# One task list for both attentions, two single score banks, and operands that change places

## The chip, the cores and the metric

The kernel runs on one core of one Trainium2 chip. The metric is device time in microseconds. The kernel before takes 2530.77 us, the median of three runs (2530.05 to 2532.8). All other times are from one profiled execution of it.

## The reference

It is one layer of a streaming encoder for 592 tokens: 512 of a prompt with 16 meta tokens in front of them, and 64 further tokens of a running stream, which also reads 128 cached positions. The model width is 2048.

```python
z = rmsnorm(x) @ w_in                       # 3904 columns, all heads
# group A, 8 heads: differential attention, two components of 64
s = q_c @ k_c.T * DIFF_SCALE + bias         # c = 0, 1; T5 relative bias
p = softmax(s_0) - lam * softmax(s_1)
o_d = rmsnorm(p @ v) * (1 - lam_init)
# group B, 8 heads: latent attention
qm  = rmsnorm(z_cq) @ w_uq                  # 128 plain + 64 rotated columns a head
km, vm = rmsnorm(z_ckv) @ w_ukv ; k_rope = rope(z_kr)
o_m = softmax((qn @ km.T + qr @ k_rope.T) * MLA_SCALE) @ vm
x = x + concat(o_d, o_m) @ w_out
x = x + (silu(h @ w_gate) * (h @ w_up)) @ w_down   # h = rmsnorm(x)
```

Attention is causal by chunks of 64. The new keys, values, latents and rotated keys are outputs too.

## The kernel before

All products of the projections and attentions are taken in three matmuls: each float32 operand is split in a high part (a copy on ScalarE, L156) and the rest (a subtraction on VectorE, L153), and high·high, high·low and low·high are summed in PSUM. A projection of 128 output columns reads its weights in two loads of 512 KB (tile `wr`, two buffers, on SP's queue), each split into `wh` and `wl` (two buffers each). Each half feeds 48 matmuls of 128x296, 6 for each of 8 slices of the width. Here "a weight half" is such a load.

**The order of the work.** `Streams` (L46) is a planner that runs while the program is written. Each task is a generator with a rank; the planner holds a clock of its own, runs the ready task of the lowest rank, and advances the clock by a guessed time for each matmul. A task that needs PSUM calls `take("sp")` (scores), `"tp"` (transposes), `"po"` (the output of an attention) or `"ps"` (projections), and hands it back with `give(name, delay)`, where the delay is a guess of when the reader will have finished. What the planner decides is TensorE's order of instructions; it is kept as written. The other engines are put in order by the scheduler of the language, and wait by semaphores, so a wrong guess costs waiting and nothing else. Tasks of low rank are attentions; the task of the highest rank is filler.

**First attention (L325 to L684).** After the norm and the bias tables (built from `oh` and `rbt`, tile `tsk`, pool `xc`), `projections()` (L616) makes queries, keys and values of head after head as filler, and `diff_attend` (L542) runs a head: five blocks of queries b (widths W of 144, 272, 400, 528, and 192 for the stream's tokens), in each the two components c. For each, two matmuls write the score tile `sp`, VectorE adds the bias and takes the minimum (L559, the "reduce" of this document, whose results are `e` and `nm`), ScalarE takes the exponential, and VectorE weighs and subtracts. The score tile is one tile of two banks, of which there is one (pool `pss`, bufs=1):

```python
pss = ph.enter_context(tc.tile_pool(name="pss", bufs=1, space=PSUM, reuse_waits="tile"))
def sbig(name="sp"):
    return pss.tile([P, 2, 512], F32, name=name, tag="sp")
...
st.give("sp", 1.2 + 0.0015 * W)
if c == 0:
    yield 1.2 + 0.0015 * W
```

Block 3 (W = 528) lies in both banks, 264 columns in each. The probabilities are transposed into `tp` and multiplied with the values into `po` (`probabilities_times_values`, L214). The head's norm uses the two-bank score tile too (`pq`). Finished heads go to memory (`mspill`). After head 7 come seven more projections, i in (4, 5, 6, 0, 1, 2, 3), for the latents; then `st.run()` at L684 ends the first list of tasks.

**Second attention (L687 to L973).** New pools are opened. SP loads the rotation matrix `rot` and the tables `cos` and `sin` (L717 to L719), POOL reloads seven heads from `mspill` (L742), and `mix_operand` splits them. `latents()` rotates the shared keys (`pr`) and splits the latents; `heads()` (L952) makes queries and keys of head after head, `latent_attend` scores them (five matmuls a piece, a maximum L928, an exponential L929), and `mix_out()` (L816), the output projection over the first eight heads, is filler. `qsum` (L748) is the sum of squares for the query norm. `mh` and `ml` are the split small weights. A second `st.run()` ends it. The rest of the output projection and the feed-forward part (L1120 to the end) follow.

Of the kernel before, what the change touches and what calls it, by code (L numbers as in the profile page):

```python
# [115 lines left out]
def encoder_step(  # L116
# [14 lines left out]
    wp_cm = tc.tile_pool(name="wp", bufs=2, reuse_waits="tile")  # L131
# [82 lines left out]
    def probabilities_times_values(pt_b, p5, pm, vm, vkeys, vown, vpast, pool, tbank, pso, pace, done, bufs, transposed):  # L214
# [21 lines left out]
        st.give("tp", 1.9)  # L236
        for t in range(2):
# [12 lines left out]
            st.give("tp", 1.9)  # L250
# [34 lines left out]
    def scores(b, sp, parts):  # L285

        if b == 4:
            n, W, q0 = NS, P + NS, 0
            pieces = [(0, 0, W, 0)]
            flat = True  # L290
        else:
            n, W, q0 = P, 144 + P * b, OWN + P * b
            flat = W <= 512
            k0 = PAST + NS
            pieces = [(0, 0, W, k0)] if flat else [(0, 0, W // 2, k0), (1, 0, W // 2, k0 + W // 2)]
        for bank, o, w, k0 in pieces:
            for i, (q, k) in enumerate(parts):
                PE.matmul(sp[0:n, bank, o:o + w], q[:, q0:q0 + n], k[:, k0:k0 + w],
                          start=i == 0, stop=i == len(parts) - 1)
        if flat:  # L300
            return n, W, sp[0:n, 0, 0:W], lambda t: t
        return n, W, sp[0:n, :, 0:W // 2], lambda t: t.rearrange("p (a b) -> p a b", a=2)

# [21 lines left out]
    with ExitStack() as ph:  # L325
        xp = ph.enter_context(tc.tile_pool(name="xp", bufs=1, reuse_waits="tile"))
        az = ph.enter_context(tc.tile_pool(name="az", bufs=1, reuse_waits="tile"))
        pj = ph.enter_context(tc.tile_pool(name="pj", bufs=2, space=PSUM, reuse_waits="tile"))
        pss = ph.enter_context(tc.tile_pool(name="pss", bufs=1, space=PSUM, reuse_waits="tile"))
        pst = ph.enter_context(tc.tile_pool(name="pst", bufs=1, space=PSUM, reuse_waits="tile"))  # L330
        pso = ph.enter_context(tc.tile_pool(name="pso", bufs=1, space=PSUM, reuse_waits="tile"))

# [3 lines left out]
        def sbig(name="sp"):  # L336
            return pss.tile([P, 2, 512], F32, name=name, tag="sp")
# [10 lines left out]
        rb = az.tile([P, T], F32, name="rb")  # L348
# [75 lines left out]
        ap = ph.enter_context(tc.tile_pool(name="ap", bufs=1, reuse_waits="tile"))  # L424

        qs = [[[ap.tile([P, T], F32R, name=f"q{i}{c}{s}") for s in "hl"] for c in range(2)] for i in range(2)]
        pt_b = [ap.tile([P, NM + P * (b + 1)], F32, name=f"p{b}") for b in range(4)]
        pmt = ap.tile([80, 512], F32R, name="pm")
        vmt = [ap.tile([80, P], F32R, name=f"vm{i}") for i in range(2)]
        for t in [pmt] + vmt:  # L430
            G.memset(f32(t), 0.0)
        p5 = ap.tile([P, 2 * P], F32, name="p5")
        G.memset(p5, 0.0)

# [12 lines left out]
        with tc.tile_pool(name="xc", bufs=1, side="right", reuse_waits="tile") as xc:  # L447
# [27 lines left out]
        zl_cm = tc.tile_pool(name="zl", bufs=1, side="right", reuse_waits="tile")  # L475
        zl = zl_cm.__enter__()
# [65 lines left out]
        def diff_attend(h, kk, vh, vl):  # L542
# [7 lines left out]
            for b in range(5):  # L550
                ls = ap.tile([P, 2], F32, name="ls", tag="ls", bufs=4)
                es = []
                for c in range(2):
                    yield from st.take("sp")
                    n, W, view, vw = scores(b, sbig(), [(q, kk[c]) for q in qs[h % 2][c]])
                    nm = ap.tile([P, 1], F32, name="nm", tag="nm", bufs=4)
                    e = ap.tile([P, 528], F32, name="e", tag="e", bufs=3)
                    bt = bias5 if b == 4 else bias[:, 528 - W:528]
                    V.tensor_tensor_reduce(  # L559
                        out=vw(e[0:n, 0:W]), in0=view, in1=vw(bt), op0=ALU.add, op1=ALU.min,  # L560
                        scale=-1.0, scalar=3e38, accum_out=nm[0:n])
                    S.activation(e[0:n, 0:W], e[0:n, 0:W], AF.Exp, bias=nm[0:n], scale=-1.0,
                                 accum_out=ls[0:n, c:c + 1])
# [10 lines left out]
                yield 1.2 + 0.0015 * W  # L574
# [6 lines left out]
            o32 = zl.tile([P, TQ], F32, name="o32", tag="o32")  # L581
# [12 lines left out]
            yield from st.take("sp")  # L594
            pq = sbig("pq")
            for i in range(2):
                c = slice(i * QH, (i + 1) * QH)
                for n, t in enumerate((sqh, sql)):
                    PE.matmul(pq[:, i, 0:QH], ones_r, t[:, c], start=n == 0, stop=n == 1)
            V.tensor_scalar(hv(sq, TQ), ev(pq, QH), 1.0 / P, EPS, op0=ALU.mult, op1=ALU.add)  # L600
# [4 lines left out]
            st.give("sp", 1.7)  # L605
# [8 lines left out]
        qsum = zl.tile([P, T], F32, name="qsum")  # L614

        def projections():  # L616
            for h in range(H):
                ps = ps0 if h == 0 else pjt()
                if h:
                    yield from project(ps, w_in[:, h * P:(h + 1) * P], xs1)  # L620
                if h >= 2:
                    yield [scored[h - 2]]
# [42 lines left out]
        def key_latents():  # L665
# [7 lines left out]
            for i in range(2):  # L673
                PE.matmul(pq[:, i, 0:TH], ones, a[:, i * TH:(i + 1) * TH], start=True, stop=True)
# [12 lines left out]
    with ExitStack() as ph:  # L687
# [169 lines left out]
        def rotary_queries(j):  # L857
# [5 lines left out]
            if j:  # L863
                yield [scored[2 * j - 1]]
# [647 lines left out]
```

## Time and profile before

| | us |
|---|---|
| median of three runs | 2530.77 |
| profiled execution | 2534.27 |
| its span | 2531.5 |
| TensorE busy | 2415.7 (95%) |
| VectorE busy | 1843.6 (73%) |
| ScalarE busy | 1142.2 (45%) |
| GpSimd busy | 758.8 (30%) |

The span goes from the first to the last recorded instruction; the profiled execution took 2.77 us beyond it. PE is TensorE, DVE VectorE, ACT ScalarE, POOL GpSimd, SP SyncE, which issues most transfers. The granted clock is TensorE's, as a share of its full one: 0.984 over the whole execution. "Busy" counts a matmul as busy also when it runs at the lower clock. By the trace the first attention runs from about 100 us to 572 us, the second from about 600 us to 900 us, and the feed-forward part fills the rest.

### The profile page before, as it was taken

Reading aid. Unit: us, or ns where it says so; the run is one execution under the profiler, and the core shown is the slowest. Engines: PE = TensorE matmul, PEld = TensorE weight load, DVE = VectorE, ACT = ScalarE, POOL = GpSimd, SP = SyncE. Lnnn points to the kernel's source line nnn. Section 1 sums busy time; section 2 is a strip of 40 time slices with the busy share of each in tenths; the row PEclk is TensorE's granted clock in tenths of the full one; section 3 lists DMA queues with packets and bytes.
Section 4 is the critical chain, followed back from the end, with each engine's and each line's share of the span. In section 5 each row is a group of like instructions: output and inputs, shape, how many; then the busy total and the mean of one; then the engine's idle time right before and its main releaser. Section 6 shows DMA issues by size and latency. Waiting matters only on the chain. (4 is left out here: it accounts for less than half of the span.)

```text
span 2531.5 us, 44317 instructions
## 1 busy us (share of the span) xinstructions
PE 2415.7 (95%) x17543; PEld 2358.5 (93%) x17543; DVE 1843.6 (73%) x2886; ACT 1142.2 (45%) x2063; POOL 758.8 (30%) x607
## 2 busy tenths in 40 slices
PE   6999999997999999999999999999999899999997
PEld 4999999997999888999999999999999899999997
DVE  5566566656666568877777777777778899999985
ACT  5344444433444444444444444444445444444445
POOL 0000000121000164644545445454543222222236
PEclk9999999998999999999999999999999999999999
DMA  7433322324332453333323334333344642452334
GB/s 207 121 91 88 86 80 81 82 84 125 102 102 85 152 160 112 124 133 119 127 100 129 126 119 138 107 118 118 124 133 152 216 156 84 151 165 84 104 105 153
DMA packets 329538, 306.43 MB, mean 121 GB/s; under 512 B 24643, under 2 KB 298442, under 8 KB 329330
## 3 DMA queue, kind: packets, MB, share of 16 engines
q1 hardware_dynamic: 328770, 301.54, 37.9%
q8 instruction: 137, 2.24, 0.4%
q0 software_dynamic: 560, 2.06, 0.2%
q14 instruction: 71, 0.58, 0.1%
HBM read 249.85 MB, written 56.39 MB: 121 GB/s over the span
## 5 line engine op out<-in xcount | busy, mean ns | idle before, releaser
L1110 PE MATMUL m<-bh,wh 128*128 128x288 f32 x3584 | 968.9, 296 | 10.2 <-ACT wh L156 10.2
L1110 PE MATMUL m<-bl,wh 128*128 128x288 f32 x3584 | 968.4, 295 | 0.0
L1110 PEld LDWEIGHTS m<-bh,wh 128*128 128x128 f32 x3584 | 675.4, 188 | 10.9 <-ACT wh L156 10.9
L1110 PEld LDWEIGHTS m<-bl,wh 128*128 128x128 f32 x3584 | 678.8, 189 | 0.1
L1114 PE MATMUL m<-bh,wl 128*128 128x288 f32 x3584 | 587.5, 299 | 14.6 <-DVE wl L153 12.6
L1114 PEld LDWEIGHTS m<-bh,wl 128*128 128x128 f32 x3584 | 512.2, 189 | 28.8 <-DVE wl L153 26.1
L1079 POOL TENSOR_TENSOR ws<-raw 128x512 f32<-128x512 f32 x256 | 341.8, 1343 | 599.7 <-DVE wl L153 305.9
L156 ACT ACTIVATE wh<-ws 128x512 fp32r<-128x512 f32 (+1 forms) x340 | 288.7, 849 | 448.1 <-PE m L1110 300.2
L153 DVE TENSOR_TENSOR wl<-ws,wh 128x512 fp32r<-128x512 f32 (+1 forms) x340 | 387.6, 1140 | 113.6 <-ACT wh L156 112.0
L153 DVE TENSOR_TENSOR wl<-raw,wh 128x512 fp32r<-128x512 f32 x416 | 403.4, 984 | 28.3 <-ACT wh L156 18.0
L156 ACT ACTIVATE wh<-raw 128x512 fp32r<-128x512 f32 x416 | 249.7, 626 | 303.0 <-PE m L1110 280.5
L108 PE MATMUL ps<-xh,wh 128*128 128x296 f32 x992 | 229.1, 313 | 5.8 <-ACT wh L156 5.8
L108 PE MATMUL ps<-xl,wh 128*128 128x296 f32 x992 | 221.0, 305 | 0.0
L108 PE MATMUL ps<-xh,wl 128*128 128x296 f32 x992 | 220.4, 304 | 0.0
L108 PEld LDWEIGHTS ps<-xh,wh 128*128 128x128 f32 x992 | 165.0, 195 | 8.9 <-ACT wh L156 6.0
L108 PEld LDWEIGHTS ps<-xl,wh 128*128 128x128 f32 x992 | 165.9, 194 | 0.4 <-DVE xl L161 0.2
L108 PEld LDWEIGHTS ps<-xh,wl 128*128 128x128 f32 x992 | 165.4, 193 | 0.3 <-DVE wl L153 0.3
L153 DVE TENSOR_TENSOR wl<-wr,wh 128x1024 fp32r<-128x1024 f32 (+1 forms) x110 | 119.4, 1086 | 51.7 <-ACT wh L156 49.6
L1079 DVE TENSOR_TENSOR ws<-ws,raw 128x512 f32<-128x512 f32 x128 | 91.3, 714 | 69.5 <-POOL ws L1079 61.6
L1349 DVE TENSOR_TENSOR y<-y,m 128x288 f32<-128x288 f32 x280 | 125.6, 449 | 19.2 <-PE m L1114 18.0
L156 ACT ACTIVATE wh<-wr 128x1024 fp32r<-128x1024 f32 (+1 forms) x110 | 101.7, 929 | 71.5 <-PE ps L108 66.3
L1257 POOL TENSOR_TENSOR c<-c,rb 128x576 f32<-128x576 f32 x44 | 73.1, 1662 | 166.5 <-ACT c L1256 166.5
(367 smaller groups left out, 3292.2 us busy)
## 6 DMA issues: line engine op xcount, KB each, us to landing
raw<-in_ffn_w_gate SPq DMA_DIRECT2D x44, 1024.0 KB, 6.6
raw<-in_ffn_w_up SPq DMA_DIRECT2D x44, 1024.0 KB, 5.4
raw<-in_ffn_w_down SPq DMA_DIRECT2D x40, 1024.0 KB, 5.7
wr<-in_w_in SPq DMA_DIRECT2D x60, 512.0 KB, 4.0
actspill<-c SPq DMA_DIRECT2D x44, 288.0 KB, 2.1
sumspill<-c SPq DMA_DIRECT2D x20, 576.0 KB, 2.8
bl<-sumspill SPq DMA_DIRECT2D x80, 144.0 KB, 3.5
bl<-actspill SPq DMA_DIRECT2D x68, 144.0 KB, 3.4
```

Of the source, the lines that this page charges most:

```text
L108: self.tc.keep_in_program_order(self.pe.matmul(out, lhsT, rhs, start=start, stop=stop))
L153: V.tensor_tensor(lo, src, f32(hi), op=ALU.subtract)
L156: S.activation(hi, src, AF.Copy)
L1079: engine.tensor_tensor(w[:, k:k + m, :], pick(xs), pick(ys), op=op)
L1110: PE.matmul(banks[p], wh[:, k, :], x, start=first and new and k == 0 and x is hi, stop=False, skip_group_check=not new)
L1114: PE.matmul(banks[p], wl[:, k, :], hi, start=False, stop=last and k == n - 1, skip_group_check=not new)
L1257: G.tensor_tensor(g[:, f, :], g[:, f, :], rb2, op=ALU.mult)
L1349: V.tensor_tensor(c, c, banks[p], op=ALU.add)
```

## The change

1. Scores are written into single banks, of which there are two (pool `psb`, bufs=2). Block 3 is cut in two pieces of 264 columns with a reduce each; in the first attention the second takes the first's minimum as its starting value, in the second attention two maxima are joined, and two exponentials summed. The tiles of the norms (`pq`, `pl`, `pr`) become two single banks with an evacuation each.
2. The guessed delays change: 2.0 + 0.0015 per column (first attention) and 2.4 + 0.002 (second) for a score bank, 2.2 in place of 1.9 for `tp`, 0.5 between components.
3. The projection tiles `ps` are taken and given through the planner during the first attention as well.
4. There is one task list. `second_part()` starts after head 7's attention, while the latent projections still run. It closes the first attention's pool `ap`, opens the operands of the second (`mx`, `mo`) in its place, loads `rot`, `cos`, `sin` and the caches, reloads the heads (on SP in place of POOL), and starts `latents()`. When the projections are done it puts the rest (`aq`) where the normalised input lay, and starts `query_latents()` and `mix_out()`.
5. Weights, input and tables lie on other sides of the memory: `wp` and `xp` to the right; the tables' pool `xc` where the raw input tiles were; `qn`, `rq`, `xo`, `rsq` and `o32` share tiles with latents that are no longer needed.
6. Small weights are loaded and split two ahead (`feed`), with two buffers for `mh` and `ml`. `queries_keys` comes before `rotary_queries`, `pair_values` after the odd head of a pair. The evacuations `pkh` and `pkl` have two buffers in place of three in the second attention.

```diff
+        pss.close()
+        bank = pss.enter_context(tc.tile_pool(name="psb", bufs=2, space=PSUM, reuse_waits="tile"))
+        zl = ph.enter_context(tc.tile_pool(name="zl", bufs=1, reuse_waits="tile"))
+        zx = ph.enter_context(tc.tile_pool(name="zx", bufs=1, reuse_waits="tile"))
+        ap_cm = tc.tile_pool(name="ap", bufs=1, reuse_waits="tile")
+        ap = ap_cm.__enter__()
...
+                cuts = [(0, W)] if W <= 512 else [(0, W // 2), (W // 2, W)]
                 for c in range(2):
-                    yield from st.take("sp")
-                    n, W, view, vw = scores(b, sbig(), [(q, kk[c]) for q in qs[h % 2][c]])
...
-                    V.tensor_tensor_reduce(
-                        out=vw(e[0:n, 0:W]), in0=view, in1=vw(bt), op0=ALU.add, op1=ALU.min,
-                        scale=-1.0, scalar=3e38, accum_out=nm[0:n])
+                    for i, (l, r) in enumerate(cuts):
+                        yield from st.take("sp")
+                        sp = sbank()
+                        for m, q in enumerate(qs[h % 2][c]):
+                            PE.matmul(sp[0:n, 0:r - l], q[:, q0:q0 + n], kk[c][:, k0 + l:k0 + r],
+                                      start=m == 0, stop=m == 1)
+                        V.tensor_tensor_reduce(
+                            out=e[0:n, l:r], in0=sp[0:n, 0:r - l], in1=bt[:, l:r], op0=ALU.add, op1=ALU.min,
+                            scale=-1.0, scalar=nm[0:n, 0:1] if i else 3e38, accum_out=nm[0:n, i:i + 1])
+                        st.give("sp", 2.0 + 0.0015 * (r - l))
...
-                    st.give("sp", 1.2 + 0.0015 * W)
-                    if c == 0:
-                        yield 1.2 + 0.0015 * W
+                    yield 0.5
...
+            st.spawn(0, second_part(), [att[H - 1]])
             for i in (4, 5, 6, 0, 1, 2, 3):
...
-        for name in ("sp", "tp", "po"):
-            st.bank(name, 1)
-        st.spawn(9, projections())
-        st.run()
...
+        def second_part():
+            yield [keyed]
+            ap_cm.__exit__(None, None, None)
+            mx = second["mx"] = ph.enter_context(tc.tile_pool(name="mx", bufs=1, reuse_waits="tile"))
+            for name, shape, src in (("rot", [P, P], c_rot), ("cos", [P, T], c_cos), ("sin", [P, T], c_sin)):
+                second[name] = mx.tile(shape, F32, name=name)
+                load(second[name], src)
...
+            for h in range(H - 1):
+                load(f32(mixl[h]), mspill[h])
+            mix_operand(H - 1, outputs[H - 1])
+            st.spawn(3, latents(cn, rn), [turned, keyed])
+            yield 3.0
+            for h in range(H - 1):
+                mix_operand(h, f32(mixl[h]))
+                yield 1.5
+            yield [projected]
+            xp_cm.__exit__(None, None, None)
+            aq.append(ph.enter_context(tc.tile_pool(name="aq", bufs=1, side="right", reuse_waits="tile")))
+            for n in range(2):
+                feed()
+            st.spawn(2, query_latents())
+            st.spawn(30, mix_out())
...
-        for h in range(H - 1):
-            G.dma_start(f32(mixl[h]), mspill[h])
...
+        for name, n in (("ps", 1), ("sp", 2), ("tp", 1), ("po", 1)):
+            st.bank(name, n)
+        st.spawn(25, projections())
         st.run()
```

**Where instructions move.** First place: TensorE, the 272-wide block of head 4. `sp` is a score tile, `kk` the split keys, `q00` and `q01` the queries of the two components (`h` and `l` their parts); `ps` is the filler projection. Before:

```order
L108 MATMUL sp<-kk_2951,q00h 128x272
L108 MATMUL sp<-kk_2951,q00l 128x272
L108 MATMUL ps<-xh_92,wh 128x296 x2
L108 MATMUL ps<-xl_108,wh 128x296 x2
L108 MATMUL ps<-xh_92,wl 128x296 x2
L108 MATMUL ps<-xh_93,wh 128x296 x2
L108 MATMUL ps<-xl_109,wh 128x296 x2
L108 MATMUL ps<-xh_93,wl 128x296 x2
L108 MATMUL ps<-xh_94,wh 128x296 x2
L108 MATMUL ps<-xl_110,wh 128x296 x2
L108 MATMUL ps<-xh_94,wl 128x296 x2
L108 MATMUL sp<-kk_2952,q01h 128x272
```

The same place in the changed kernel:

```order
L108 MATMUL sp<-kk_2976,q00h 128x272
L108 MATMUL sp<-kk_2976,q00l 128x272
L108 MATMUL ps<-xh_92,wh 128x296 x2
L108 MATMUL ps<-xl_108,wh 128x296 x2
L108 MATMUL ps<-xh_92,wl 128x296 x2
L108 MATMUL sp<-kk_2977,q01h 128x272
L108 MATMUL sp<-kk_2977,q01l 128x272
```

The second component's matmuls come 6 filler matmuls after the first's, where 18 stood. From there to the second 264-wide piece of block 3 stand 42 filler matmuls in the new order.

Second place: VectorE, where the keys of head 5 are taken out of PSUM (`z`) while head 4's scores run; `o` is a head's output being normalised, `kk` the stacked keys, `na` the keys in their natural order on the way to memory. Before:

```order
L559 ISA e,nm<-sp,bias 128x272
L559 ISA nm 128x1
L168 SCALAR_TENSOR_TENSOR sq<-sq,r 128x576
L632 TENSOR_TENSOR z<-ps,rb 128x592
L169 SCALAR_TENSOR_TENSOR r<-sq,r 128x576
L153 TENSOR_TENSOR wl<-wr,wh 128x1024
L602 SCALAR_TENSOR_TENSOR o_3257<-o_3257,gT,r 128x576
L517 TENSOR_TENSOR kk_3535<-z,kk_3535 64x592
L517 TENSOR_TENSOR kk_3536<-z,kk_3536 64x592
L559 ISA e,nm<-sp,bias 128x272
```

In the changed kernel (the first component's reduce stands just ahead of these rows):

```order
L633 TENSOR_TENSOR z<-ps,rb 128x592
L169 SCALAR_TENSOR_TENSOR r<-sq,r 128x576
L553 ISA e,nm<-sp,bias 128x272
L553 ISA nm 128x1
L596 SCALAR_TENSOR_TENSOR o_3243<-o_3243,gT,r 128x576
L505 TENSOR_TENSOR kk_3566<-z,kk_3566 64x592
L505 TENSOR_TENSOR kk_3567<-z,kk_3567 64x592
L561 RECIPROCAL ls<-ls 128x2
L473 COPY na<-pna 128x512
L562 TENSOR_TENSOR ls<-ls,lamv 128x2
L553 ISA e,nm<-sp,bias 128x400
```

The second component's reduce now stands ahead of `o` and the two `kk`, and a weight split `wl` has moved behind them.

Third place: SP's queue of transfers at the seam between the two attentions. Before:

```order
L137 DMA wr<-in_w_in 128x8x128 x6
L137 DMA cn<-in_cache_mla_ckv 128x256
L137 DMA rn<-in_cache_mla_krope 128x64 x2
L137 DMA wr<-in_w_out 128x8x128 x3
L137 DMA rot<-c_rot 128x128
L137 DMA cos<-c_cos 128x592
L137 DMA sin<-c_sin 128x592
```

In the changed kernel:

```order
L137 DMA wr<-in_w_in 128x8x128 x7
L137 DMA rot<-c_rot 128x128
L137 DMA cos<-c_cos 128x592
L137 DMA sin<-c_sin 128x592
L137 DMA cn<-in_cache_mla_ckv 128x256
L137 DMA rn<-in_cache_mla_krope 128x64 x2
L137 DMA mxl_5866<-mspill 128x576
L137 DMA mxl_5867<-mspill 128x576
```

`rot` has moved ahead of the first weights of the output projection and stands right behind the last weight half of the input projection; the reloads of the heads follow it. On TensorE the rotation that uses it (`pr`) came after all input projections; it now stands in the middle of the next-to-last one, behind 30 of the 48 matmuls of its first weight half:

```order
L108 MATMUL ps<-xh_96,wh 128x296 x2
L108 MATMUL ps<-xl_112,wh 128x296 x2
L108 MATMUL ps<-xh_96,wl 128x296 x2
L108 MATMUL pr<-zl_5514,rot 128x296 x2
L108 MATMUL ps<-xh_97,wh 128x296 x2
L108 MATMUL ps<-xl_113,wh 128x296 x2
```

At the program's start, finally, the loads of `oh` and `rbt` stood ahead of the third weight load on SP and now stand behind the last store of the transposed input (`xspill`).

More of the change, by code (lines that the diff above doesn't have):

```diff
@@ L283, in probabilities_times_values @@
         st.give("po", 1.0)
[L285 to L302, printed above, removed]
     def ev(ps, n=TH):
@@ L774, in latents @@
             split(rkh[:, PAST:TP], rkl[:, PAST:TP], kr)
-            for i in range(4):
-                split_scaled(cqh[i], cql[i], zs[i], gq[:, i:i + 1])
-            yield from st.take("ps")
-            pq = pjt()
-            for i in range(2):
-                PE.matmul(pq[:, i, 0:TH], ones, qsum[:, i * TH:(i + 1) * TH], start=True, stop=True)
-            v = ztile("v")
-            V.tensor_scalar(hv(v), ev(pq), 1.0 / QL, EPS, op0=ALU.mult, op1=ALU.add)
-            rsqrt(rsq, v)
-            st.give("ps", 1.5)
-        def latent_rows():
+            yield 3.0
             for j in range(5):
```

352 lines of the change are left out of this document (196 added, 156 removed).

## The prediction

> **What bounds the kernel now.** I read the page's busy line first, then the busy time by stage (a row: from and to, length, busy us and instructions of PE, PEld, DVE, ACT and POOL, granted clock, DMA share, GB/s), then TensorE's waits in each stage.
>
> ```profile
> PE 2415.7 (95%) x17543; PEld 2358.5 (93%) x17543; DVE 1843.6 (73%) x2886; ACT 1142.2 (45%) x2063; POOL 758.8 (30%) x607
> 100.00:572.00 472.00, 445.88 (x3199) 437.28 (x3198) 287.96 (x593) 206.41 (x417) 24.42 (x30) 0.98 0.30 84
> 572.00:600.00 28.00, 14.51 (x60) 11.51 (x60) 22.35 (x28) 13.42 (x22) 5.62 (x3) 0.63 0.43 127
> 600.00:842.00 242.00, 238.99 (x1754) 231.28 (x1754) 145.50 (x308) 102.39 (x224) 9.77 (x15) 1.00 0.30 93
> 842.00:900.00 58.00, 51.37 (x343) 46.64 (x342) 34.74 (x60) 27.96 (x55) 21.58 (x19) 0.94 0.65 198
> ```
>
> TensorE is the bound, and the number of its matmuls hardly changes. So a gain can only come from time in which it stood still or ran at a lower clock. I call that a stage's loss: idle time plus busy time times (1 − clock).
>
> - First attention, 100 to 572: idle 472 − 445.9 = 26.1, clock 445.9 × 0.02 = 8.9; loss 35.
> - The seam between the phases, 572 to 600: idle 13.5, clock 14.5 × 0.37 = 5.4; loss 18.9.
> - Second attention, 600 to 842: loss 3.0.
> - Its end, 842 to 900: idle 6.6, clock 51.4 × 0.06 = 3.1; loss 9.7.
>
> The change touches nothing after that but what these stages hand on. TensorE's waits, for the first two stages and the end:
>
> ```profile
> PE sp L108 <- DVE nm L559: 21.2, 16, 2.5
> PE tp L112 <- DVE pk2l L153: 4.9, 5, 1.7
> ...
> PE ps L108 <- DVE ml L153: 4.6, 1, 4.6
> PE pr L108 <- DMA rot<-c_rot: 3.5, 1, 3.5
> PE ps L108 <- ACT mh L156: 3.2, 1, 3.2
> PE ps L108 <- POOL qsum L748: 2.3, 1, 2.3
> ...
> PE tp L112 <- DVE pm L233: 1.8, 1, 1.8
> PE tp L112 <- DVE pk0l L153: 1.1, 1, 1.1
> ```
>
> (waited for: us in total, times, longest.) Of 26.1 us idle in the first attention, 21.2 is one thing: a score matmul waits until the reduce on VectorE has read the one score tile. In the seam four waits in a row make 13.6, all on things that could be ready earlier.
>
> **Two score banks, first attention.** One such wait, on VectorE and TensorE, in head 4:
>
> ```profile
> 337.26 0.77 DVE L632 TENSOR_TENSOR z<-ps,rb 128x592 f32<-128x592 f32 x1
> 337.94 0.75 DVE L169 SCALAR_TENSOR_TENSOR r<-sq,r 128x576 f32<-128x576 f32 x1
> 338.61 1.22 DVE L153 TENSOR_TENSOR wl<-wr,wh 128x1024 fp32r<-128x1024 f32 x1
> 339.75 0.81 DVE L602 SCALAR_TENSOR_TENSOR o<-o,gT,r 128x576 f32<-128x576 f32 x1
> 340.59 1.57 DVE L517 TENSOR_TENSOR kk<-z,kk 64x592 fp32r<-64x592 f32 x2
> 342.19 0.44 DVE L559 CUSTOM_DVE_ANT_0 e<-sp,bias 128x272 f32<-128x272 f32 x1
> 342.56 0.69 DVE L485 COPY na<-pna 128x512 f32<-128x512 f32 x1
> 343.44 0.57 DVE L559 CUSTOM_DVE_ANT_0 e<-sp,bias 128x400 f32<-128x400 f32 x1 [0.20 <-PE sp L108]
> 344.33 0.36 DVE L570 TENSOR_SCALAR e<-e,ls 128x272 f32<-128x272 f32 x1
> 344.73 0.50 DVE L572 SCALAR_TENSOR_TENSOR p<-e,ls 128x272 f32<-128x272 f32 x1
> ...
> 342.69 0.45 PE L108 MATMUL sp<-kk,q00h 128*128 128x400 f32 x1 [1.93 <-DVE nm L559]
> ...
> 342.00:344.00 2.00, 1.31 (x6) 1.30 (x7) 1.77 (x7) 0.62 (x2) 0.00 (x0) 0.77 1.01 325
> 344.00:346.00 2.00, 2.00 (x10) 2.00 (x10) 1.13 (x6) 0.72 (x2) 0.00 (x0) 0.50 0.50 162
> 346.00:348.00 2.00, 2.00 (x14) 1.94 (x14) 0.17 (x1) 1.08 (x2) 0.00 (x0) 0.87 0.04 8
> ```
>
> The reduce of the second component lies behind 5.1 us of other VectorE work (z to kk); TensorE waits 1.93 us, and then its clock falls: 1.31 × 0.23 + 2.00 × 0.50 + 2.00 × 0.13 = 1.6 us more.
>
> In the new order the second component's two matmuls come 6 projection matmuls after the first's, where 18 stood, so its reduce goes ahead of o and kk on VectorE. With two banks a piece waits only for the reduce two pieces back. Is that always early enough? The tightest place is the second piece of 264 in block 3, which needs the bank of the 400-wide score of component 1. Matmul spacing comes from here:
>
> ```profile
> 573.06 0.44 PE L108 MATMUL ps<-xh,wh 128*128 128x296 f32 x2
> 573.34 0.43 PE L108 MATMUL ps<-xl,wh 128*128 128x296 f32 x2
> ```
>
> Two take 0.27, one 0.137 us; a weight half (48) takes 6.6. Between the 272 score of component 1 and that piece stand 42 of them, 5.8 us, and with the scores and transposes between (an estimate of 0.9 from the same spacing) 6.6. VectorE's queue over that stretch, from the rows above: reduce 0.44, o 0.81, kk 1.57, small steps 0.2, na 0.69, reduce 0.57, 0.36, 0.50, a weight split 1.22 and the reduce awaited 0.57, together 6.9, starting about 0.4 after its matmul. So a wait of 0.7 stays where 1.93 and 1.6 were lost. Added on VectorE per head: two more pieces to reduce and one more evacuation. Two rows give the fixed part (0.57 − 0.44 for 128 columns, so 0.13 of a reduce does not scale), hence some 0.4 us a head; VectorE is 61% busy in the stage (288 of 472), which covers it, except inside the burst, where it is part of that 0.7.
>
> What remains, per head: 0.7 here, 0.8 for transposes (4.9 + others over some 8 heads), 0.3 small; 1.8 × 8 = 14, and 3 at a lower clock, since waits below a microsecond are not followed by a slow stretch in the rows I have. Loss 17, **gain 18**. Bounds: 35 if all goes; 0 if each wait only moves; I take the middle because the big waits go and the small ones stay. Its own range is 8 to 28.
>
> On the clock, in sentences that the sum does without: in this case a wait of 1.93 was followed by half clock. [...]
>
> **The seam.** Latent keys, their rotation and the splits of the eight heads' outputs now start while projections still run, so the four waits of 13.6 lose their cause, but a new one appears. In the new order the rotation `pr` stands on TensorE 30 projection matmuls, 4.1 us, into the fourth weight half from the end (call its start c). Its matrix `rot` is loaded behind the last weight half on SP; that load needs the raw buffer of the half two before, so it waits for that half's split:
>
> ```profile
> 567.25 1.06 ACT L156 ACTIVATE wh<-wr 128x1024 fp32r<-128x1024 f32 x1 [5.50 <-PE ps L108]
> 568.34 1.23 DVE L153 TENSOR_TENSOR wl<-wr,wh 128x1024 fp32r<-128x1024 f32 x1 [5.33 <-ACT wh L156]
> ...
> 577.50 1.28 PE L108 MATMUL pr<-zl,rot 128*128 128x296 f32 x4 [3.45 <-DMA rot<-c_rot]
> ...
> wr<-in_w_in SPq DMA_DIRECT2D x60, 512.0 KB, 4.0
> mr<-in_mla_w_uq SPq DMA_DIRECT2D x48, 64.0 KB, 2.6
> mxl<-mspill POOLq DMA_DIRECT2D x7, 288.0 KB, 5.9
> ```
>
> 1.06 + 1.23 and two steps of 0.75 queued on VectorE (z and r, above) put it at c + 3.7. `rot` has 64 KB, but shares the engines with the 512 KB just ahead: between 2.6 and 4.0, I take 4.0, so c + 8. TensorE waits 4 (1.5 to 6), and everything is behind it: the filler projections are in the same queue. By the ratio at 342 (1.6 lost to the clock for 1.93 idle) come 3.3 more, so 7.3. Small waits (first bank swap, first output tile) I put at 2.5. Loss 9.8 against 18.9: **gain 9** (2 to 16). The seven reloads go from POOL to SP and their splits to ScalarE ahead of the last weight split. At the 198 GB/s of the end stage 7 × 288 KB take 10.4 us, and cos, sin and the caches ahead of them (some 780 KB) 4; from c + 8 that is c + 22, and with the last half's split c + 24. TensorE wants that half after three halves (19.7), the 7.3 and the rest of the seam, about c + 29: covered by 5.
>
> **Start.** The tables `oh` and `rbt` now lie where input tiles were; so SP loads them behind the last store of x.
>
> ```profile
> 55.63 2.06 SPq L140 DMA_DIRECT2D xspill<-xt  x4
> 60.40 1.02 PE L108 MATMUL ptr<-oh,rbt 32*8 32x512 f32 x1 [0.87 <-DVE rb L445]
> ```
>
> The stores are issued by 57.7; the tables then at 57.8 to 58.5, landing after 2.6 to 4.0: 60.4 to 62.5 against a use at 60.40. **Loss 1** (0 to 3).
>
> **Second attention and its end.** Block 3 needs one more reduce, a min, an exp and an add per head. VectorE is 60% busy there (145.5 of 242) and output-projection matmuls fill: 1 lost (−5 to +2 in gain, since only 3.0 can come back). At the end some 30 filler matmuls (4 us) now lie between the last transposes, whose waits are 1.8 + 1.1; but the x tiles come from other buffers and weight splits cluster: +4 − 3 = 1 (−4 to +5).
>
> **Sum**: 18 + 9 − 1 − 1 + 1 = 26. The profiled run took 2534.27 with a span of 2531.5, so it lies 3.5 above the median run; taken off the span that is 2505.5, and off the median of 2530.77 it is 2505. I predict 2505.
>
> **Rivals.**
>
> 1. `rot` is in time: the half's split goes ahead on VectorE and the load lands by c + 4.5. Then the 7.3 goes too: 2498. For: 64 KB loads take 2.6. Against: it waited 3.45 in this very place. Chance 0.18.
> 2. Reloads and splits pile up on SP and ScalarE, so that the last weight half's split comes 10 later: the cover of 5 is gone, TensorE waits 5 and loses 3 to the clock: 2513. For: a median of 5.9 for a reload of 288 KB now. Against: the estimate of 10.4 above. Chance 0.15.
> 3. Only idle time comes back, and the clock losses recur elsewhere: 18 becomes 12, so 2511. For: 114 to 116, after a wait of 2.10, ran at full clock (below). Against: 344 to 346 at half. Chance 0.10. [...]
>
> ```profile
> 112.63 0.39 PE L108 MATMUL sp<-kk,q01h 128*128 128x272 f32 x1 [2.10 <-DVE nm L559]
> 114.00:116.00 2.00, 2.00 (x16) 2.00 (x15) 1.20 (x5) 0.87 (x3) 0.00 (x0) 1.00 0.00 0
> ```
>
> 4. Slower. The two-piece block 3 is the place: if VectorE reaches the 400-wide reduce 2.6 later than reckoned (two weight splits of 1.22 in the burst instead of one), the second piece waits 0.7 + 2.6 = 3.3, the clock falls (1.6), and the norm's second bank waits behind it (1.1): 6.0 a head, 48 over eight heads against 35 now. That is 13 lost, with +8 elsewhere 5 lost: 2536. It decides from a lateness of about 2: (0.7 + 2 + 1.6 + 0.1 small) × 8 = 35. For: TensorE never has more than 42 filler matmuls of cover there. Against: a split recurs once in 6.6 us of TensorE time, so two seldom meet. Chance 0.08.
> 5. The second bank does nothing, each wait moving to the next piece: 18 falls to 0, 2523. For: VectorE's burst of 5.1 us is the same. Against: no piece needs the bank of the reduce just behind it. Chance 0.05.
>
> **Numbers.** The forecast itself has 0.44 (its own range 2495 to 2514). A measurement tells 0.2%, 5 us, from no change: 2525.7 is the edge. Faster: 0.44 + 0.18 + 0.15 + 0.10 = 0.87; no change: rival 5, 0.05; slower: rival 4, 0.08. The range reaches from the good bounds of the two main gains (28 and 16, the rest at nothing: 2487) over rival 2 with the worst of the end stage (2513 + 5 + 3): 2521. Outside lie rivals 4 and 5 and a little beyond.
>
> **What would show it.** Right: from 100 to 572 the same work ends about 18 us earlier with score waits below 5 us in total; `pr` waits about 4 us for `rot`; no four-wait seam. Wrong: score waits above 15 us, or a low clock in most heads (rivals 4, 5); a wait of TensorE for ScalarE's `wh` in the last half (rival 2); idle time down but the clock loss still 9 (rival 3).

## The result, and the profile after

The changed kernel takes 2499.56 us (median of four runs, 2497.23 to 2504.32) beside 2530.41 for the kernel before on the same chip: a ratio of 0.9879, with a 95% interval of 0.9862 to 0.9896. That is 31 us faster; 2505 had been forecast, with 26 us. Two of the ten executions of the run with a raised guess (below) were in a slow state of the chip, at 4699 and 4761 us, and its median leaves them out.

Below are the page's busy line of the changed kernel and its busy time by stage (columns as in the prediction). The stages are cut where they answer those before: the start (0 to 106), first attention (106 to 526), the seam (526 to 574), second attention (574 to 800), and its end (800 to 900).

```profile
PE 2401.5 (96%) x17543; PEld 2349.8 (94%) x17543; DVE 1840.0 (74%) x2957; ACT 1142.4 (46%) x2079; POOL 751.6 (30%) x600
...
0.00:60.00 60.00, 38.52 (x204) 31.93 (x204) 31.32 (x63) 35.49 (x79) 1.26 (x8) 0.91 0.66 198
60.00:106.00 46.00, 42.12 (x286) 40.56 (x287) 19.41 (x31) 12.92 (x22) 0.14 (x1) 0.93 0.58 160
106.00:526.00 420.00, 409.83 (x3008) 402.51 (x3007) 277.04 (x627) 201.97 (x413) 10.68 (x19) 1.00 0.31 87
526.00:574.00 48.00, 43.36 (x287) 40.67 (x286) 33.27 (x40) 17.14 (x26) 13.51 (x11) 0.93 0.56 166
574.00:800.00 226.00, 220.06 (x1608) 213.28 (x1608) 146.25 (x338) 103.42 (x241) 8.73 (x12) 0.99 0.32 98
800.00:832.00 32.00, 28.92 (x192) 27.11 (x191) 11.92 (x19) 11.27 (x22) 0.00 (x0) 0.89 0.44 142
832.00:900.00 68.00, 64.53 (x457) 61.06 (x456) 42.93 (x73) 31.46 (x61) 41.90 (x36) 1.00 0.54 165
```

The start of the kernel before, which the prediction did not show:

```profile
0.00:60.00 60.00, 38.01 (x205) 30.89 (x205) 32.51 (x68) 35.59 (x80) 1.27 (x8) 0.94 0.69 203
60.00:104.00 44.00, 42.83 (x292) 40.55 (x293) 18.11 (x26) 12.71 (x21) 0.15 (x1) 0.92 0.56 166
```

TensorE executes the same number of matmuls as before (17543). Loss is again idle time plus busy time at the missing clock:

| stage | loss before | loss after | gained | forecast |
|---|---|---|---|---|
| start | 23.2 idle + 5.7 clock = 28.9 | 25.4 + 6.4 = 31.8 | −2.9 | −1 |
| first attention | 26.1 + 8.9 = 35.0 | 10.2 + 0 = 10.2 | 24.8 | 18 |
| seam | 13.5 + 5.4 = 18.9 | 4.6 + 3.0 = 7.6 | 11.3 | 9 |
| second attention | 3.0 + 0 = 3.0 | 5.9 + 2.2 = 8.1 | −5.1 | −1 |
| its end | 6.6 + 3.1 = 9.7 | 6.6 + 3.2 = 9.8 | −0.1 | 1 |
| sum | | | 28.0 | 26 |

A stage does not hold the same matmuls in both (the seam has 60 before and 287 after), so the table compares what was lost and not the lengths. The spans of these two executions differ by 34.4 (2531.5 and 2497.1). The 6.4 that the table leaves are not located: the clock is read to two digits (0.005 of the 446 us busy in the first attention is already 2.2), and what lies behind 900 us is not in the table. The medians differ by 30.9, since the profiled execution before lay 3.9 above its median and the one after 0.3 below.

TensorE's waits in the changed kernel, first attention, seam and second attention:

```profile
PE sp L108 <- DVE nm L553: 5.1, 7, 0.9
PE tp L112 <- DVE pk2l L153: 3.3, 4, 0.8
PE pnb L112 <- DVE na L473: 1.1, 1, 1.1
...
PE pr L108 <- DMA rot<-c_rot: 4.3, 1, 4.3
PE pn L112 <- DVE cl L153: 0.3, 1, 0.3
...
PE pv L108 <- DVE vm L207: 2.1, 1, 2.1
PE sp L108 <- ACT e L961: 1.2, 2, 0.8
PE sp L108 <- DVE rq L886: 0.8, 2, 0.5
```

The score waits fell from 21.2 us in 16 to 5.1 in 7. Of the four waits of the seam one is left, the forecast one for `rot`. In the second attention a new wait of 2.1 stands for `pv`, the transposition bank of the value rows.

### The profile page after: what moved, and what is told of

It is laid out like the page before. It is cut to its first block, busy times and chain, and to the rows that moved or that the text cites. A ratio compares the mean times of both kernels' runs of the same rounds, so it can differ in the third digit from the quotient of the medians.

```text
span 2497.1 us, 44396 instructions
## 1 busy us (share of the span) xinstructions
PE 2401.5 (96%) x17543; PEld 2349.8 (94%) x17543; DVE 1840.0 (74%) x2957; ACT 1142.4 (46%) x2079; POOL 751.6 (30%) x600
```

## The experiments

Ratios are to the kernel before, run beside each; the changed kernel has 0.9879.

**One part alone: two score banks in the kernel before.** The score loop of the first attention, `pq` and `pl` are the changed kernel's, with their guessed delays, so that TensorE's order changes with the banks; all else is the kernel before.

```diff
+        bank = pss.enter_context(tc.tile_pool(name="psb", bufs=2, space=PSUM, reuse_waits="tile"))
...
-                    n, W, view, vw = scores(b, sbig(), [(q, kk[c]) for q in qs[h % 2][c]])
+                    for i, (l, r) in enumerate(cuts):
+                        yield from st.take("sp")
+                        sp = sbank()
...
-        for name in ("sp", "tp", "po"):
-            st.bank(name, 1)
+        for name, n in (("sp", 2), ("tp", 1), ("po", 1)):
+            st.bank(name, n)
```

> The kernel before with one part of the change alone: in the first attention, scores and norm sums use two single banks (block 3 in two pieces, the new guessed delays for these banks). Two task lists, seam, tables and second attention stay as before. Theory: the second score bank is what the first attention gains by, some 25 of the 31 us, so 2503 to 2508; waits of TensorE for the reduce fall from 21.2 us to below 7, and no stretch at low clock stays between 104 and 560. Rival: the gain of that stage needs the single list (projection tiles taken through the planner, other places in memory): then 2520 or more and score waits above 12.

Measured: 2506.45, ratio 0.9898 (0.988 to 0.9916), about 26 of the 31 us. First attention and seam of this run, and its waits:

```profile
104.00:548.00 444.00, 433.43 (x3179) 425.84 (x3178) 286.31 (x634) 205.49 (x417) 22.09 (x30) 1.00 0.32 90
548.00:576.00 28.00, 15.53 (x58) 11.85 (x58) 23.53 (x30) 13.02 (x22) 7.92 (x5) 0.63 0.37 104
...
PE sp L108 <- DVE nm L571: 5.1, 7, 0.9
PE ps L108 <- DVE ml L153: 4.6, 1, 4.6
```

The stage's loss is 10.6, as in the changed kernel, with the same seven score waits. The seam is that of the kernel before, 12.5 idle at a clock of 0.63, with a wait of 4.0 for `rot`. So the gain of the first attention needs nothing of the single list; the theory stands.

**Only the bank taken away.** The first try held the second bank by a second tile that nothing writes, once with the planner reckoning with it, once without (TensorE's order then that of the changed kernel).

```diff
+                        yield from st.take("sp")
                         sp = sbank()
+                        sbank("idle")
...
-                        st.give("sp", 2.0 + 0.0015 * (r - l))
+                        for _ in range(2):
+                            st.give("sp", 2.0 + 0.0015 * (r - l))
```

> The changed kernel with only the second score bank taken away in the first attention: each piece occupies both banks (the second is left unused), and the planner reckons with it. Theory: some 22 to 27 us are lost, 2522 to 2527; score waits of 15 us or more are back, half of them followed by a stretch at low clock. Rival (order and single list carry the gain): not above 2508.

> As the one-bank run, but the planner still believes in two banks, so TensorE's order is exactly that of the changed kernel. It tells the bank from the order. Theory (an order that places the second component 6 matmuls behind the first only pays if the bank is there): each of the ten score pieces of a head now waits about a reduce, 1 to 2 us, and the burst 5: some 10 us a head with the clock, 80 in all, so 2560 to 2600. Rival (the new order itself helps): below 2530.

Measured: 2519.75, ratio 0.9958 (0.9939 to 0.9976), and 2502.24 in a single run. The second has the very waits of the changed kernel, 5.1 us in seven, and in the first a score waits for the reduce two pieces back, not one (that at 304.82 for the reduce begun at 304.27, whose score was written before the one at 303.27): the unwritten tile took no bank. So neither is what its expectation says. The second repeats the changed kernel. The first is a run with two banks and an order with wider gaps, and tells something else. Its first attention and seam:

```profile
106.00:526.00 420.00, 409.20 (x3003) 403.84 (x3002) 275.80 (x604) 195.35 (x396) 14.87 (x20) 1.00 0.31 87
526.00:600.00 74.00, 53.81 (x341) 48.83 (x341) 44.84 (x71) 27.76 (x48) 10.06 (x10) 0.82 0.40 120
...
PE pn L112 <- DVE cl L153: 14.7, 1, 14.7
```

The stage itself is as good, but the heads' chains are longer, so head 7 ends late, the projections run out as filler, and the seam loses 20.2 idle and 9.7 by its mean clock (an upper bound, since the clock was low from 553 to 580 us and the wait of 14.7 lies in that stretch). Here spacing scores further apart was paid for at the end of the filler, with those 14.7.

The second try gives the first attention a pool of one bank for each of two names and uses one name until the projections are done. TensorE's order is that of the changed kernel.

```diff
-            return bank.tile([P, 512], F32, name=name, tag="sp")
+            if not projected["done"]:
+                return bank.tile([P, 512], F32, name=name, tag="sp0")
+            turn[0] += 1
+            return bank.tile([P, 512], F32, name=name, tag=f"sp{turn[0] % 2}")
...
-        bank = pss.enter_context(tc.tile_pool(name="psb", bufs=2, space=PSUM, reuse_waits="tile"))
+        bank = pss.enter_context(tc.tile_pool(name="psb", bufs=1, space=PSUM, reuse_waits="tile"))
```

> The changed kernel with one score bank for all of the first attention and the seam (the second bank lies idle until the projections are done), while TensorE's order is exactly that of the changed kernel. It does what the same-order run was meant to do: that one showed the changed kernel's waits unchanged, since a tile that nothing writes takes no bank. Theory (the order pays only with the bank): the second component's score, 6 matmuls (0.8 us) behind the first, waits for a reduce each time, and in the burst for all of it: some 10 us a head, 2560 to 2600. Rival (the order is what helps): below 2510.

Measured: 2553.83, ratio 1.0086 (1.0068 to 1.0103). From 106 to 526:

```profile
106.00:526.00 420.00, 375.27 (x2653) 360.22 (x2652) 248.58 (x559) 183.40 (x376) 4.79 (x15) 0.99 0.28 79
...
PE sp L108 <- DVE nm L558: 37.3, 35, 3.6
```

54 us slower than the changed kernel and slower than before: the new order without the bank is worse than the old one. It is somewhat below the 2560 to 2600 expected: a score waits 1.1 on the mean (37.3 by 35), not 1 to 2, and the clock stays at 0.99.

**A better guess in place of a bank.** In the kernel before only the planner's guess for the wide score tile is raised.

```diff
-                    st.give("sp", 1.2 + 0.0015 * W)
+                    st.give("sp", 3.0 + 0.0015 * W)
```

> The kernel before with one number changed: the planner's guess of when the one wide score tile is free again goes from 1.2 to 3.0 us (plus 0.0015 per column), so that more filler stands between scores. It tells whether the waits came from a wrong guess or from the lack of a bank. Theory (bank): the score waits fall, but each head's chain of ten scores gets some 15 us longer and the filler runs out at the last heads, as in the one-bank run that only moved the order (14.7 us in one wait at the seam): 2520 to 2540. Rival (guess): the 30 us at stake in that stage come back without a bank, 2500 to 2512.

Measured: 2534.06 (median of eight), ratio 1.0014 (1.0004 to 1.0025). Waits, and the stages to 560, 600 and 860:

```profile
PE sp L108 <- DVE nm L559: 16.2, 15, 1.6
...
106.00:560.00 454.00, 435.50 (x3132) 428.92 (x3131) 280.15 (x579) 199.61 (x404) 16.80 (x23) 0.97 0.29 84
560.00:600.00 40.00, 24.61 (x99) 18.83 (x97) 27.02 (x38) 20.04 (x34) 9.34 (x10) 0.68 0.38 119
600.00:860.00 260.00, 249.75 (x1795) 239.24 (x1795) 156.49 (x328) 110.54 (x241) 9.63 (x16) 0.98 0.32 98
```

The score waits shrink a little, but the stage still loses 31.6 (18.5 idle and 13.1 by the clock) of the 35.0 before. The seam loses 15.4 idle and 7.9 to the clock, and what follows to 860 loses 15.2 more, where the kernel before lost 18.9 and then 12.7 up to 900. This guess alone brings no gain; others were not tried.

**The wait for `rot`.** `rot`, `cos` and `sin` are issued from ScalarE's queue.

```diff
-                load(second[name], src)
+                S.dma_start(second[name], src)
```

> The changed kernel with rot, cos and sin issued from ScalarE's queue in place of SP's, where they stand behind the last weight half; TensorE's order is unchanged. Theory: the wait of 4.3 us for rot and the 2.5 us at low clock behind it go, save up to 1: 2492 to 2495. Rival: the next thing in line (the last weight half, its split, or sin and the rotated keys) takes the wait over: 2497 or more.

Measured: 2493.23, ratio 0.9848 (0.983 to 0.9866), 6 us below the changed kernel. The seam, and ScalarE's queue:

```profile
526.00:574.00 48.00, 45.05 (x307) 42.96 (x306) 35.40 (x42) 17.81 (x26) 14.36 (x11) 0.96 0.60 178
...
524.07 0.39 ACTq L699 DMA_DIRECT2D rot<-c_rot  x1
...
528.23 1.16 PE L108 MATMUL pr<-zl,rot 128*128 128x296 f32 x4
533.20 0.30 PE L112 MATMUL pkr<-ident,rn 128*128 128x128 f32 x1 [1.36 <-DMA rn<-in_cache_mla_krope]
```

`rot` is issued at 524.07, not 529.21, and `pr` starts without a wait. Part of the wait moves on: 1.36 for `rn`, which is still on SP, and 1.6 for the latents' split. The seam's loss goes from 7.6 to 4.8 (3.0 + 45 × 0.04); another 1.7 are the low clock behind `pv`, which this run has not, and in which the edit has no part (last section). The rest of the 6 is not located.

**GpSimd beside the weight split.** The sums of squares of latent 1 are done with those of latent 2.

```diff
-                elif i < 4:
+                for m in ((1, 2) if i == 2 else (3,) if i == 3 else ()):
                     t = ztile("t")
-                    G.tensor_tensor(t, zs[i], zs[i], op=ALU.mult)
+                    G.tensor_tensor(t, zs[m], zs[m], op=ALU.mult)
```

> The changed kernel with GpSimd's squares and sum for latent 1 done together with those of latent 2, so that GpSimd is idle while VectorE splits the weight half whose raw buffer the last half waits for. In the changed kernel that split takes 2.20 us beside GpSimd (1.23 elsewhere), and rot's load is issued behind it. Theory: the split takes 1.23 again, rot is issued and arrives about 1 us earlier: the wait of 4.3 becomes 3.3, time 1 to 1.5 less, 2498. Rival: the split is slow for another reason (transfers), and the wait stays 4.3.

Measured: 2494.86, ratio 0.9855 (0.984 to 0.9869), 4.7 us less, where 1 to 1.5 were expected. The two operations on VectorE and those of GpSimd, changed kernel first, this run's below:

```profile
526.52 2.20 DVE L153 TENSOR_TENSOR wl<-wr,wh 128x1024 fp32r<-128x1024 f32 x1
528.64 1.99 DVE L596 SCALAR_TENSOR_TENSOR o<-o,gT,r 128x576 f32<-128x576 f32 x1
526.02 1.62 POOL L669 TENSOR_TENSOR t<-zl 128x592 f32<-128x592 f32 x1 [13.95 <-DVE zl L663]
527.72 2.30 POOL L670 TENSOR_TENSOR qsum<-qsum,t 128x592 f32<-128x592 f32 x1
```

```profile
527.84 1.21 DVE L153 TENSOR_TENSOR wl<-wr,wh 128x1024 fp32r<-128x1024 f32 x1
528.98 0.81 DVE L596 SCALAR_TENSOR_TENSOR o<-o,gT,r 128x576 f32<-128x576 f32 x1
PE pr L108 <- DMA rot<-c_rot: 3.2, 1, 3.2
```

The mechanism is as expected: the split takes 1.21 again, and the wait for `rot` is 3.2, not 4.3. Of the 4.7 the trace shows this 1.1, 1.2 less at low clock behind it (1.8 against 3.0), and 1.7 behind `pv`, where the edit has no part (last section). The 1.2 need not be its doing either: in the run for `pv` below, the wait for `rot` is 4.1, and the clock of the seam is 0.96, as in this run. The rest is not located.

**The tables early.** The tables' pool goes to the right side.

```diff
-        with tc.tile_pool(name="xc", bufs=1, reuse_waits="tile") as xc:
+        with tc.tile_pool(name="xc", bufs=1, side="right", reuse_waits="tile") as xc:
```

> The changed kernel with the tables' tiles (oh, rbt, trs, the lambda rows) on the right side of the memory, not where the raw input lay, so that SP loads them early as before; TensorE's order is unchanged. The start lost 3.6 us against the kernel before: TensorE waits 3.0 us for the copy trs, 0.8 before. Theory: the late loads make VectorE do trs after two query splits and the lambda product; early loads give 2 to 3 us back: 2496.5 to 2498. Rival: the loss of the start is spread over a run's own differences, and nothing comes back: 2499 to 2500.

Measured: 2499.26, ratio 0.9871 (0.9856 to 0.9886): not told apart from the changed kernel. TensorE's second table matmul, changed kernel first:

```profile
65.23 0.64 PE L108 MATMUL ptr<-oh,rbt 32*8 32x144 f32 x2 [3.01 <-DVE trs L432]
```

```profile
64.19 0.64 PE L108 MATMUL ptr<-oh,rbt 32*8 32x144 f32 x2 [0.77 <-DVE trs L432]
60.00:106.00 46.00, 44.36 (x302) 42.68 (x302) 19.68 (x27) 12.75 (x22) 0.14 (x1) 0.93 0.56 167
```

The 2.2 us of idle came back as the theory said (1.6 in place of 3.9 in the stage), but the time does not show it. In this execution the first 60 us lost 22.3 idle and 4.1 to the clock (0.89), against 21.5 and 3.5 in the changed kernel, so some 1.5 of the 2.2 went there. The run with `rot`, which leaves the start as it was, has that clock of 0.89 too, and 2 us are near what the runs spread by.

**Lateness in the burst.** Three more operations per head stand ahead of `o` on VectorE (their result is their input).

```diff
             rsqrt(r, sq)
+            for _ in range(3):
+                V.scalar_tensor_tensor(r, r, 1.0, r, op0=ALU.mult, op1=ALU.max)
```

> The changed kernel with three more VectorE operations of 0.75 us in each head's norm, just ahead of o in the burst: the reduces behind come 2.25 us later, and nothing else is changed (TensorE's order is the same). The prediction's slower rival said that from a lateness of 2 us the second piece of block 3 waits 2.7 and the clock falls: 4 to 5 us a head, 35 in all, 2530 or more. The other theory (two banks with 42 filler matmuls between have that slack, since the reckoned wait of 0.7 was already too high: 5.1 us of score waits over all heads were measured): about 0.5 to 1.5 us a head, 2504 to 2512, and no low clock.

Measured: 2525.74, ratio 0.9971 (0.9957 to 0.9984), 26 us slower than the changed kernel. From 106 to 526:

```profile
106.00:526.00 420.00, 392.21 (x2846) 385.03 (x2845) 282.62 (x635) 194.16 (x401) 8.35 (x18) 0.99 0.30 83
...
PE sp L108 <- DVE nm L553: 15.1, 8, 2.7
PE pnb L112 <- DVE na L473: 9.1, 5, 3.1
...
340.99 1.22 DVE L153 TENSOR_TENSOR wl<-wr,wh 128x1024 fp32r<-128x1024 f32 x1
342.54 1.22 DVE L153 TENSOR_TENSOR wl<-wr,wh 128x1024 fp32r<-128x1024 f32 x1
343.68 0.57 DVE L553 CUSTOM_DVE_ANT_0 e<-sp,bias 128x400 f32<-128x400 f32 x1
344.31 0.39 PE L108 MATMUL sp<-kk,q00h 128*128 128x264 f32 x1 [2.44 <-DVE nm L553]
```

Neither size fits, but the slower rival's place and wait do: the delay brings a second weight split ahead of the 400-wide reduce, and the second 264-wide piece waits 2.44 to 2.7. That is not all of the loss, though. This execution took 2521.6, 22.3 more than the changed kernel's. Score waits are 10.0 us more than in the changed kernel (15.1 against 5.1), and 8.0 more stand for the keys' transposes (`pnb`, 9.1 against 1.1), which the rival did not have. The clock takes 4 to 5, by three low stretches in eight heads, where the rival had one in each. It is 3.3 us a head in all, where the rival had 4 to 5 and the other theory at most 1.5. In this burst the two banks have no slack left: 2.25 us added on VectorE cost 2.2 us of idle a head (27.8 in the stage against 10.2).

**The wait for `pv`.** The planner's guess for the first bank of the value rows goes from 1.6 to 4.0.

```diff
-                st.give("tp", 1.6)
+                st.give("tp", 1.6 if i else 4.0)
```

> The changed kernel with the planner's guess for the first transposition bank of pair_values raised from 1.6 to 4.0, so that more filler stands before the second. In the changed kernel TensorE waits 2.08 us there once (for the copy vm behind a weight split on VectorE) and loses 1.6 us to the clock after it. Theory: 3 to 4 us come back, 2496. Rival: the filler spent there is missing at the second attention's end, where the waits grow by as much: 2499 to 2500.

Measured: 2498.33, ratio 0.9866 (0.9851 to 0.9881), not told apart from the changed kernel. Second attention and the first part of its end:

```profile
574.00:800.00 226.00, 222.65 (x1656) 217.77 (x1655) 147.35 (x337) 103.03 (x241) 8.28 (x12) 1.00 0.32 98
800.00:832.00 32.00, 26.68 (x156) 23.10 (x155) 12.04 (x21) 12.19 (x23) 0.00 (x0) 0.84 0.46 149
```

The stage's loss goes from 8.1 to 3.4, but that of the next from 6.3 to 9.6: filler spent on the one wait is missing at the other, as the rival had it.

**Three edits together**: `rot` from ScalarE's queue, the deferred sums, the early tables.

> The changed kernel with three of the edits together: rot, cos, sin from ScalarE's queue, GpSimd's sums of latent 1 deferred, and the tables on the right side. Theory: the first gives 6; the second saves 1 at rot's load alone, which no longer counts, and the 1.2 us of o; the third 2 of idle at the start: 2489 to 2493. Rival: each of them only moved a wait that the others have too, and it is no better than the first alone: 2493 to 2495.

Measured: 2491.75, ratio 0.9846 (0.9828 to 0.9863). It is faster than the kernel before and the changed one, but not told apart from the run with `rot` alone. The seam:

```profile
526.00:574.00 48.00, 46.21 (x325) 44.04 (x325) 37.04 (x46) 19.84 (x29) 14.04 (x11) 1.00 0.61 180
```

Its loss is 1.8, of 18.9 in the kernel before.

## Why the prediction was right, and where its terms were off

- **Two score banks: mechanism right, size too small** (18 forecast, 24.8 measured, inside 8 to 28). The wait of 0.7 at the second piece of block 3 is there, but not in all heads: 0.8 in four and 0.2 in a fifth, 3.4 us where 0.7 in each of eight had been reckoned; two others, of 0.9 and 0.8, bring the score waits to 5.1. Of the remainder of 14 idle and 3 clock, 10.2 and 0 were measured. Two terms were too high: 0.8 a head for transposes occurs in four heads, not eight, and the 0.3 a head for small waits hardly occurs; and no low clock is left at all. The fixed part of a reduce was misread (0.13 is what 128 columns more cost; by the same two rows the fixed part is 0.44 − 272 × 0.13 / 128 = 0.16), which hardly changes the 0.4 a head. The second bank is shown to be the cause from both sides: with the order made for it, it gives 26 us in the kernel before, and without it that order loses 54. Two banks under the old order were not run.
- **The seam: right** (9 forecast, 11.3 measured). `pr` waits 4.30 for `rot` against 4, and loses 3.0 to the clock against 3.3. The term of 2.5 for small waits was too high, 0.3 is left. The cover for reloads and splits held, and rival 2 did not occur. That the wait is so near 4 is partly luck: the split before the load began 0.7 earlier than reckoned (c + 1.8 by the trace, not c + 2.5), and GpSimd's sums, which the reckoning lacked, made it 1.0 longer (2.2, not 1.2).
- **The start: sign right, cause half right** (−1 forecast, −2.9 measured). The late loads themselves did not delay the first table matmul, which waits 0.87 for `rb` as before. VectorE's queue was ordered anew around them: the copy `trs` stands behind two query splits and the lambda product. The early tables take those 2.2 away.
- **Second attention: mis-sized** (−1 forecast, −5.1 measured). The step failed where it said that only 3.0 us were at stake, and took the added reduces as its cost. The cost is one wait of 2.1 for the copy `vm`, behind a weight split, with a low clock behind it (1.7 by the rows of the last section; the table's 2.2 comes of the rounded clock), and 2.0 of score waits. That `pair_values` moved to another place in the order was read and not priced.
- **The end: 0 for 1.** As the run for `pv` shows, filler there is what the second attention has not used.
- **The sum.** That 28.0 is so near 26 is partly luck: two stages gave 9.1 more than forecast and three 7.1 less.
- **Rivals.** `rot` in time (2498) is nearest by the time, but by the trace it did not occur: its 7.3 us are lost, and the gain came from the banks. The clock rival is refuted here: it let only the idle part of the 18 come back (12, which is 26.1 less the 14 that were to stay), but removing the score waits of about 2 us took the stage's clock loss from 8.9 to 0, beside 15.9 of idle. The slower rival did not occur, but its place was right: with 2.25 us more on VectorE the second piece of block 3 waits as it said, though that wait is only part of the 3.3 us a head. The fifth, that the second bank does nothing, is out.

## What to carry to other kernels

When TensorE waits for the reader of its one result bank, price a second bank by the worst burst on the reader's engine and not by its mean load (here 61% busy, and in the burst 2.25 us more on VectorE cost 2.2 us of idle a head). Here an order written for two banks was worse than the old one without the second (2553.83 us, 1.0086 of the kernel before), and spacing the scores further apart was paid when the filler ran out (14.7 us in one wait). A transfer that is moved earlier can still wait for what stands ahead of it in its queue (here `rot`, behind the last weight half, was issued at 529.21 us, and from ScalarE's queue at 524.07), so look which engine frees the buffer of the load before it, and consider another engine's queue.

## What the runs showed of the hardware

**The clock price of one and the same wait.** The wait for `pv` is 2.08 in the changed kernel and 2.09 in the run with `rot` on ScalarE's queue. Around it, changed kernel first:

```profile
603.24:606.65 3.41, 1.32 (x11) 1.12 (x10) 3.24 (x7) 1.06 (x4) 0.00 (x0) 1.00 0.58 163
606.65:610.06 3.41, 3.41 (x17) 3.41 (x17) 1.20 (x5) 1.31 (x5) 0.00 (x0) 0.50 0.78 240
```

```profile
598.11:601.53 3.42, 2.51 (x21) 2.28 (x19) 3.35 (x7) 2.50 (x5) 0.00 (x0) 1.00 0.36 114
601.53:604.94 3.41, 2.24 (x17) 2.27 (x18) 2.18 (x8) 1.42 (x6) 0.00 (x0) 1.00 0.60 162
604.94:608.35 3.41, 3.41 (x30) 3.41 (x29) 1.63 (x6) 0.78 (x3) 0.23 (x1) 1.00 0.40 133
```

One lost 1.7 us at half clock, the other nothing. The trace shows what differs. In these executions the low stretches begin on a grid of 3.41 us: in the first attention of the kernel before they begin at 162.19, 288.48, 343.10, 397.71 and 452.32 us, which lie 37, 16, 16 and 16 times 3.413 apart, and each lasts 3.41 (the first 6.83). The stretches above are cut on the grid of their own run. In the changed kernel the whole wait lies in one of them (2.1 idle), and the next runs at half clock. In the run with `rot` a line of the grid at 601.53 cuts the wait into 0.9 and 1.2, and the clock stays. The same holds in the kernel before: the wait of 1.93 that ended at 342.69 lay within one stretch (339.69 to 343.10); one of 1.99 from 502.93 was cut at 503.52, and no low clock followed. In its first attention each of the five stretches that were idle for 1.92 us or more was followed by half clock, and none of those up to 1.65 was. The idle time alone does not settle it everywhere: at the end of the changed kernel's second attention, the stretch from 818.28 to 821.69 was idle for 1.33 us only, and half clock followed.

So a wait of about 2 us cost its own length (1.99 in the kernel before, 2.09 in the run with `rot`) or 1.7 us more (1.93 in the kernel before, 2.08 in the changed one), by where it fell on the grid. That a few us between two runs can come from that alone is an estimate from these four. No wait of at most 1.1 us in the first attention of the changed kernel was followed by a low clock. The grid lies at another place of the span in each of the three: less whole steps of 3.413 us it is at 1.8 in the kernel before (343.10), at 2.5 in the changed one (606.65) and at 0.8 in the run with `rot` (601.53).

**VectorE and GpSimd side by side.** In the changed kernel the weight split took 2.20 us beside GpSimd's two operations, not 1.21, and `o` 1.99, not 0.81; GpSimd's product and sum took 1.62 and 2.30 beside them, and 1.18 and 1.88 in the run that deferred them. So here both got longer together, and the delay went when these operations no longer met. It was not always both: further on in the changed kernel a weight split took 2.47 from 549.96, and the sum beside it, from 549.50, took 1.84. How the two engines hold each other up, no run shows.
